# A hybrid decoder step on one core: the opening (norm, adaLN, first projections, gates) in another sequence

## The chip, the cores and the metric

The kernel runs on one core of one Trainium2 chip. The metric is device time in microseconds of one execution. The core has five engines that each work through their own queue of instructions in order: PE (matrix products), DVE and ACT (elementwise work, PSUM reads), POOL (elementwise work in SBUF) and SP (here it only issues DMAs). They wait for each other through semaphores.

## What is computed

One decoder layer over 576 tokens: a prompt of 512 and 8 samples of 8 tokens. Cut to what matters here:

```
mod = silu(c) @ ada_w + ada_b                  # 6 x 1024 per sequence
sh1, sc1, g1, sh2, sc2, g2 = split(mod, 6)
hn = rmsnorm(x, norm1_w) * (1 + sc1) + sh1
u = hn @ w_in       # z, xbc, dt, q, k, v, o, ig, fg, xr, gr
xbc = silu(causal_conv(xbc))                   # width 4
y_ssd = SSD(xbc, dt), y_ml = mLSTM(q, k, v, ig, fg), y_lru = RG-LRU(xr, gr)
x = x + g1 * (concat(y_ssd, y_ml, y_lru) @ w_out)
hn2 = rmsnorm(x, norm2_w) * (1 + sc2) + sh2
x = x + g2 * (square(relu(hn2 @ mlp_up)) @ mlp_down)
y = rmsnorm(x, final_norm_w)
```

## The kernel before

All activations lie with features on the 128 partitions: `x` is 8 tiles of 128 x 576 (k = 0..7). A float32 product is made of three fast ones: each operand is split into a high part (rounded on ACT) and a low part (the rest, on DVE or POOL), and PE adds hi·hi, lo·hi and hi·lo. With two halves of 288 columns this is 6 matmuls per weight block of 128 columns and per k; below, **product (i, k)** means these six, for the i-th of the first three weight blocks (i = 0, 1, 2 are convolution channels 8, 10 and 0) and tile k. Weight blocks are numbered in their order of use: 0 is the gates' `wg`, 1 to 3 are those three, and from 4 on each block is one *unit* of 8 products.

`start` (the opening) is recorded inside `in_order`, so on each engine its instructions stand in the order of the program text; what comes after is placed by the scheduler. The opening does this:

- Loads on SP's queue: x, the first part of `vec` (small constants), then for each q the adaLN weights `ada[q]` (four DMAs of 256 KB), with the weight blocks between them.
- Sums of squares: ACT and DVE square the x tiles, DVE adds two squares, PE sums them over the partitions (`sum_tokens`, into `ms`); warm-up matmuls (`warm`) stand between. `rstd_cols` makes the norm's factor on DVE and POOL, `rstd_bcast` (tiles `ba`, `bb`, then `rb`) spreads it.
- For each q: `ada_mm(q)` on PE (tile `adap`), a copy on ACT (`adarow`), `ada_sel(q)` on PE (tile `adas`), an add on DVE (`modt`). Then `modulate(q)` on DVE, ACT and POOL (`amp`, `x`, `hnh`, `hnl`) gives the normed tile `hn[q]` as high and low part.
- The products (i, k) in the order of the table `TODO`, with `ada_sel` and `ada_mm` of later tiles between them.
- The gates (`gates_mm`): 32 matmuls of 32 columns over the x tiles (line 429), copies `gs` on DVE and ACT, two products with a selector (line 435), then `ev_gates` (`gv` on DVE, `ic` on ACT). The convolution channels follow: `ev_conv` copies PSUM to SBUF on ACT (lines 611 to 614), ACT takes the first tap (line 620), DVE the other three (line 626), ACT and DVE the SiLU (lines 649, 651, 653; tile `xbc`).

`w_prep(b)` splits weight block b: high part `wh` on ACT, low part `wl` on DVE (on POOL for blocks 7 to 32); block 3 is split in two halves (`wt`). A unit needs a pair of PSUM banks out of two (`PG`), so unit b waits for the copies of unit b - 2. `PREP_AT` says at which k blocks 2, 3 and 4 are split.

## Time and profile before

| | |
|---|---|
| three runs | 995.92, 998.04, 1000.73 us; median 998.04 us |
| the profiled execution | 995.4 us, of which the span of the trace is 993.6 us |
| PE: span 0 to 62 us | 56.14 us busy, mean granted clock 0.92 |
| PE: 62 to 100 us | 37.08 of 38 us busy, clock 1.00 |
| DVE: 62 to 100 us | 35.95 of 38 us busy |
| PE: 100 to 150, 150 to 200, 200 to 250 us | 41.92, 46.55, 45.37 of 50 us busy |
| PE: 500 to 900 us | 400 of 400 us busy |
| DMA: 0 to 40 us | busy share 0.63 in the first 5 us, then about 1 |

The span is what the profiler recorded from the first to the last instruction; 1.8 us of the execution lie around it. The table is read by stage: the opening has PE idle time and a clock below 1, the stretch to some 300 us has waits on PE, and from 500 us on PE is busy all the time, so that what comes later shifts with the moment at which it begins.

### The profile page before, as it was taken

What the parts mean: (1) busy time and instruction counts of PE and PEld (TensorE: products, weight loads), DVE (VectorE), ACT (ScalarE), POOL (GpSimd) and SP (SyncE); (2) the same over time, 40 slices, a digit from 0 to 9 for tenths busy, and PEclk for the clock granted to TensorE, in tenths of its full rate; (3) what the DMA queues carried; (4) which work ended last, traced back from release to release, by engine and by line L of the source; (5) the groups of instructions that cost most, each with busy time, mean ns of one, the idle gap of its engine ahead of it and who ended that gap; (6) DMA issues with size and microseconds to landing.
All of it is one profiled execution on the core that took longest, in us unless ns stands there. A gap on an engine that the chain in (4) does not pass through costs nothing.

```text
span 993.6 us, 18146 instructions
## 1 busy us (share of the span) xinstructions
PE 959.5 (97%) x7369; PEld 904.1 (91%) x7370; DVE 590.2 (59%) x1180; ACT 399.8 (40%) x741; POOL 203.8 (21%) x220
## 2 busy tenths in 40 slices
PE   8999789889999999999999999999999999999996
PEld 5889778777788899999999999999999999999996
DVE  4669897887788377468444455533553355335544
ACT  3454744453646674345222234312441144114320
POOL 2836454532355532020000000000000000000032
PEclk8999999998999999999999999999999999999998
DMA  9721254654464333444222322222222222222202
GB/s 343 294 86 64 81 186 133 246 173 137 131 223 153 105 137 129 140 131 162 91 98 105 110 86 84 74 79 84 85 86 85 86 85 76 76 83 85 85 23 96
DMA packets 51220, 119.62 MB, mean 120 GB/s; under 512 B 6956, under 2 KB 17468, under 8 KB 51136
## 3 DMA queue, kind: packets, MB, share of 16 engines
q1 hardware_dynamic: 47024, 111.06, 32.7%
q10 hardware_dynamic: 3744, 6.85, 1.8%
q8 instruction: 58, 0.95, 0.4%
q0 software_dynamic: 368, 0.55, 0.2%
q14 instruction: 26, 0.21, 0.1%
HBM read 108.68 MB, written 9.76 MB: 119 GB/s over the span
## 4 chain that ended last, share of the span: by engine, by line
PE 76%; DVE 10%; ACT 4%; issue 3%; DMA 1%; POOL 0%; POOLq 0%; DVEq 0%; ACTq 0%
PE g L164 66%; DVE r L626 3%; PE adap L218 1%; PE g L1363 1%; DMA nmb<-scr_nm 1%; PE py L729 1%; PE lg L1129 1%; DVE att L707 1%; PE ps L734 1%; PE py L732 1%; DVE nmb L924 1%; DVE xbc L651 0%; DVE sp_e L494 0%; PE adas L228 0%; ACT r L620 0%
## 5 line engine op out<-in xcount | busy, mean ns | idle before, releaser
L150 ACT ACTIVATE wh<-raw 128x1024 fp32r<-128x1024 f32 x123 | 130.1, 1058 | 333.9 <-PE g L164 309.4
L164 PE MATMUL g<-hnh,wh 128*128 128x288 f32 x688 | 153.1, 302 | 10.1 <-ACT r L614 8.0
L164 PE MATMUL g<-hnh,wl 128*128 128x288 f32 x688 | 152.1, 299 | 0.6 <-DVE wl L152 0.6
L164 PE MATMUL g<-hnl,wh 128*128 128x288 f32 x688 | 151.8, 299 | 0.0
L152 DVE TENSOR_TENSOR wl<-raw,wh 128x1024 fp32r<-128x1024 f32 x97 | 118.7, 1225 | 29.5 <-ACT wh L150 29.4
L164 PEld LDWEIGHTS g<-hnh,wh 128*128 128x128 f32 x688 | 110.4, 189 | 19.3 <-ACT r L614 9.2
L164 PEld LDWEIGHTS g<-hnh,wl 128*128 128x128 f32 x688 | 111.6, 189 | 2.7 <-issue 1.2
L164 PEld LDWEIGHTS g<-hnl,wh 128*128 128x128 f32 x688 | 111.7, 189 | 0.8 <-issue 0.4
L164 PE MATMUL g<-h2h,wh 128*128 128x288 f32 (+1 forms) x512 | 110.9, 297 | 0.0
L164 PE MATMUL g<-h2l,wh 128*128 128x288 f32 (+1 forms) x512 | 110.9, 298 | 0.0
L164 PE MATMUL g<-h2h,wl 128*128 128x288 f32 (+1 forms) x512 | 110.0, 296 | 0.0
L307 DVE SCALAR_TENSOR_TENSOR xr<-g,modt,xr 128x288 f32<-128x288 f32 x38 | 19.7, 518 | 141.2 <-PE g L164 141.2
L164 PE MATMUL g<-hh,wl 128*128 128x288 f32 x480 | 102.9, 295 | 0.0
L164 PE MATMUL g<-hh,wh 128*128 128x288 f32 x480 | 102.5, 295 | 0.0
L164 PE MATMUL g<-hl,wh 128*128 128x288 f32 x480 | 102.4, 295 | 0.0
L1405 POOL TENSOR_SCALAR xr<-xr,vec 128x576 f32<-128x576 f32 (+2 forms) x8 | 15.2, 1900 | 383.8 <-ACT sqa L1237 363.4
L152 POOL TENSOR_TENSOR wl<-raw,wh 128x1024 fp32r<-128x1024 f32 x26 | 69.0, 2653 | 80.3 <-ACT wh L150 61.4
L164 PEld LDWEIGHTS g<-h2h,wl 128*128 128x128 f32 x512 | 83.4, 188 | 0.0
L164 PEld LDWEIGHTS g<-h2h,wh 128*128 128x128 f32 x512 | 83.1, 189 | 0.1
L164 PEld LDWEIGHTS g<-h2l,wh 128*128 128x128 f32 x512 | 83.0, 188 | 0.0
L164 PEld LDWEIGHTS g<-hh,wh 128*128 128x128 f32 x480 | 77.0, 188 | 0.0
L164 PEld LDWEIGHTS g<-hh,wl 128*128 128x128 f32 x480 | 77.0, 188 | 0.0
(399 smaller groups left out, 1652.7 us busy)
## 6 DMA issues: line engine op xcount, KB each, us to landing
raw<-w SPq DMA_DIRECT2D x124, 512.0 KB, 3.5
ada<-ada SPq DMA_DIRECT2D x32, 512.0 KB, 5.6
ada<-ada SPq DMA_DIRECT2D x32, 256.0 KB, 5.9
cumb<-scr_cum SPq DMA_DIRECT2D x16, 256.0 KB, 5.6
s<-s SPq DMA_DIRECT2D x16, 256.0 KB, 4.7
ssm_s<-s ACTq DMA_DIRECT2D x16, 256.0 KB, 2.9
x<-x SPq DMA_DIRECT2D x8, 288.0 KB, 4.7
xr<-x SPq DMA_DIRECT2D x8, 288.0 KB, 3.9
```

The source lines that it names most:

```text
L150: nc.scalar.activation(hi, raw, AF.Copy)
L152: eng.tensor_tensor(lo, raw, hi.bitcast(FT), op=OP.subtract)
L164: self.nc.tensor.matmul(pg.h[h][:m, :e], w(k), xx[:, h * HALF:h * HALF + e], start=start and n == 0, stop=stop and n == 2)
L218: nc.tensor.matmul(ps[32 * j:32 * j + 32, :256], self.cs[:, k, :], ks(k), start=k < 4, stop=k >= 4)
L307: self.nc.vector.scalar_tensor_tensor(dst[:, :HALF], pg.h[0][:, :HALF], gate[:, 0:1], x[:, :HALF], op0=OP.mult, op1=OP.add)
L626: nc.vector.scalar_tensor_tensor(a[:, :n], r[:, j:j + n], wcols[:, j:j + 1], a[:, :n], op0=OP.mult, op1=OP.add)
L707: self.eng("att").tensor_scalar(E[:, h * 128:(h + 1) * 128], cums[h2][:, h * 128:(h + 1) * 128], self.col1[:, c, hd:hd + 1], 0.0, op0=OP.a ...
L729: nc.tensor.matmul(o, xdt[:, h * 64:(h + 1) * 64], att[h // 4][:, hs], start=True, stop=not c)
L732: nc.tensor.matmul(o, S[:, h * 64:(h + 1) * 64], ce[h // 4][:, hs], start=False, stop=True)
L734: nc.tensor.matmul(pst, cb[:, 128:256], xend[:, :512], start=True, stop=True)
L924: self.eng("nmb").tensor_scalar(E[:, tk(c)], nmb[:, tk(c)], ecol(c), 0.0, op0=OP.add, op1=OP.min)
L1405: self.eng("fin").tensor_scalar(x, x, self.v("fnw")[:, o:o + 1], None, op0=OP.mult)
```

## The change

`start` is written in another order; no operation on the data is new except how the last pair of squares is summed.

- The last two squares (k = 6 and 7) are not added on DVE: both go to PE as sums of their own. Of 36 warm-up matmuls 24 are left: 14, 4, 4 and 2, where before there were 14, 4, 4, 4, 4 and 6.
- `rstd_cols` stands ahead of the tanh of the adaLN input; the `cs` operand is made after it.
- The split of block 1 stands ahead of `rstd_bcast`, on ACT's and on DVE's queue.
- `ada_mm` runs one q further than the product at hand instead of two, and `ada_sel(k + 1)` with `modulate(k + 1)` now stand in iteration k, behind its first product.
- Loads: `wg` and the second part of `vec` move behind all adaLN weights; blocks 1, 2 and 3 move ahead.
- `TODO` takes the channel-0 products in other portions; block 2, 3 and 4 are split one k earlier each.
- `ev_conv` of channel 8 stands behind product (0, 7), ahead of the gates; on PE the gates' second step stands further back, inside unit 5.

```diff
-            for q in range(PAIR_AT):
+            self.hn, rows = [None] * KT, {}
+            w0 = self.w_raw_gates()
+            for q in range(KT):
                 load(q)
-                self.w_load(W_AT.get(q, 0))
+                self.w_load(W_AT.get(q, -1))
+                if q == VEC_AT:
+                    nc.sync.dma_start(self.vec[:, NV1:], io["vec"][:, NV1:])
+                    w0()
...
-                nc.vector.tensor_tensor(sb, sa, sb, op=OP.add)
+                if k == KT - 2:
+                    self.sum_tokens(sa, ms, False, False)
+                else:
+                    nc.vector.tensor_tensor(sb, sa, sb, op=OP.add)
                 self.sum_tokens(sb, ms, k == 0, k == KT - 2)
-                if k < KT - 2:
+                if k < KT - 4:
                     self.warm(WARM[1])
+            r = self.rstd_cols(ms, 1.0 / D, EPS)
             th = self.rpool.tile([128, 8, 32], FT, name="cth", tag="r")
...
-            r = self.rstd_cols(ms, 1.0 / D, EPS)
...
+            self.warm(WARM[2])
             ada_mm(0)
-            self.w_prep(0)
...
+            self.w_prep(1)
             rb = self.rstd_bcast(r)
-            self.warm(WARM[2])
-            self.ada_sel(0, rows[0])
-            self.hn = [None] * KT
-            self.hn[0] = self.modulate(x[0], rb, 0)
-            self.w_prep(1)
-            self.warm(WARM[3])
+            modulation(0)
             ada_mm(1)
-            self.ada_sel(1, rows[1])
-            ada_mm(2)
             pgs = [self.PG(), self.PG(), PairTile(banks=[self.P("g"), self.P("g")])]
             for k in range(KT):
-                if k + 1 < KT:
-                    self.hn[k + 1] = self.modulate(x[k + 1], rb, k + 1)
-                if k in PREP_AT:
-                    self.w_prep(2 + PREP_AT.index(k))
...
                     if n == 0:
+                        if k + 1 < KT:
+                            modulation(k + 1)
                         if k + 2 < KT:
-                            self.ada_sel(k + 2, rows[k + 2])
-                        if k + 3 < KT:
-                            ada_mm(k + 3)
-            if not GATES_FIRST:
-                ps = self.gates_mm(x)
+                            ada_mm(k + 2)
+                        if k in PREP_AT:
+                            self.w_prep(2 + PREP_AT.index(k))
+                        if k == KT - 1:
+                            self.ev_conv(pgs[0], 8)
+            ps = self.gates_mm(x)
             self.ev_gates(ps)
-            self.ev_conv(pgs[0], 8)
...
+    def w_raw_gates(self):
+
+        t = self.T("wg")[:, :256]
+        self.w_split[0] = t.rearrange("p (k m) -> p k m", k=8)
+        self.w_next_dma = self.w_next_split = 1
+        return lambda: self.nc.sync.dma_start(t, self.io["wg"])
...
-WARM = 14, 4, 4, 6
-PAIR_AT = 3
-W_AT = {0: 1, 2: 2, 4: 3}
+WARM = 14, 4, 2
+W_AT = {0: 1, 1: 2, 3: 3}
 VEC_AT = 7
-PREP_AT = 1, 3, 6
...
+PREP_AT = 0, 2, 5
```

`modulation(q)` is `ada_sel(q)` followed by `modulate(q)`. In `TODO` the products of channel 0 (i = 2) stood two at each of k = 4 to 7; now they stand at k = 3 to 7 as one, two, two, two and one.

**PE at the first products.** This is PE's queue of before, up to the first product (0, 0) (tile `g_341`, high part `hnh_297`): `adap` is one adaLN step's product (four rows), `adas` its selection.

```order
L218 MATMUL adap_315<-ada_118,cs 32x256 x2
L218 MATMUL adap_315<-ada_119,cs 32x256 x2
L218 MATMUL adap_315<-ada_120,cs 32x256 x2
L218 MATMUL adap_315<-ada_121,cs 32x256 x2
L228 MATMUL adas_326<-vec,adarow_324 128x9 x2
L218 MATMUL adap_330<-ada_126,cs 32x256 x2
L218 MATMUL adap_330<-ada_127,cs 32x256 x2
L218 MATMUL adap_330<-ada_128,cs 32x256 x2
L218 MATMUL adap_330<-ada_129,cs 32x256 x2
L164 MATMUL g_341<-hnh_297,wh_304 128x288 x2
L164 MATMUL g_341<-hnl_298,wh_304 128x288 x2
L164 MATMUL g_341<-hnh_297,wl_305 128x288 x2
```

And this is the same place of the change, where the first product is `g_316` with `hnh_298`, and the rows behind it are iteration 0's.

```order
L216 MATMUL adap_305<-ada_117,cs 32x256 x2
L216 MATMUL adap_305<-ada_118,cs 32x256 x2
L216 MATMUL adap_305<-ada_119,cs 32x256 x2
L216 MATMUL adap_305<-ada_120,cs 32x256 x2
L162 MATMUL g_316<-hnh_298,wh_274 128x288 x2
L162 MATMUL g_316<-hnl_299,wh_274 128x288 x2
L162 MATMUL g_316<-hnh_298,wl_275 128x288 x2
L226 MATMUL adas_326<-vec,adarow_314 128x9 x2
L216 MATMUL adap_343<-ada_127,cs 32x256 x2
L216 MATMUL adap_343<-ada_128,cs 32x256 x2
L216 MATMUL adap_343<-ada_129,cs 32x256 x2
L216 MATMUL adap_343<-ada_130,cs 32x256 x2
```

The selection of tile 1 and the product of adaLN step 2 moved from ahead of product (0, 0) to behind it; the next product, (0, 1), needs that selection.

**ACT at the end of the opening.** ACT's queue of before from the split of blocks 5 and 6 (`wh_764`, `wh_768`) over the gates to the copies and the first tap of channel 8 (`g_341` is its PSUM).

```order
L150 ACTIVATE wh_764<-raw_756 128x1024
L150 ACTIVATE wh_768<-raw_758 128x1024
L433 ACTIVATE gs_693<-gp_676 128x288
L477 ACTIVATE ic_699<-gp_675,vec 4x288
L477 ACTIVATE ic_699<-gp_676,vec 4x288
L611 ACTIVATE r_707<-g_341 128x288
L613 ACTIVATE r_707<-g_341 128x224
L614 ACTIVATE r_707<-g_341 128x8x8
L620 ACTIVATE r_713<-r_707,cwh 128x600
```

The same place of the change: blocks 5 and 6 are `wh_754` and `wh_758`, channel 8 is `g_316`, channel 10 `g_317`.

```order
L148 ACTIVATE wh_754<-raw_746 128x1024
L611 ACTIVATE r_656<-g_316 128x288
L613 ACTIVATE r_656<-g_316 128x224
L614 ACTIVATE r_656<-g_316 128x8x8
L148 ACTIVATE wh_758<-raw_748 128x1024
L620 ACTIVATE r_662<-r_656,cwh 128x600
L611 ACTIVATE r_713<-g_317 128x288
```

The copies of channel 8 stand ahead of the gates, between two weight splits.

**DVE at the same place.** DVE's queue of before from the low parts of blocks 5 and 6 to the taps of channels 8 (`r_713`) and 10 (`r_729`).

```order
L152 TENSOR_TENSOR wl_765<-raw_756,wh_764 128x1024
L152 TENSOR_TENSOR wl_769<-raw_758,wh_768 128x1024
L432 COPY gs_693<-gp_675 128x288
L475 TENSOR_SCALAR gv_698<-gp_675,vec 64x288
L475 TENSOR_SCALAR gv_698<-gp_676,vec 64x288
L645 TENSOR_SCALAR cwh<-vec 128x60
L626 SCALAR_TENSOR_TENSOR r_713<-r_707,cwh,r_713 128x600 x2
L626 SCALAR_TENSOR_TENSOR r_729<-r_723,cwh,r_729 128x600
```

And of the change, with channel 8 as `r_662`, channel 10 as `r_719` and channel 0 as `r_735`.

```order
L150 TENSOR_TENSOR wl_759<-raw_748,wh_758 128x1024
L626 SCALAR_TENSOR_TENSOR r_662<-r_656,cwh,r_662 128x600 x2
L626 SCALAR_TENSOR_TENSOR r_719<-r_713,cwh,r_719 128x600
L626 SCALAR_TENSOR_TENSOR r_662<-r_656,cwh,r_662 128x600
L626 SCALAR_TENSOR_TENSOR r_719<-r_713,cwh,r_719 128x600 x2
L651 SCALAR_TENSOR_TENSOR xbc_669<-r_656,r_662 128x512
L653 SCALAR_TENSOR_TENSOR xbc_669<-r_656,r_662 128x64
L432 COPY gs_702<-gp_684 128x288
L626 SCALAR_TENSOR_TENSOR r_735<-r_729,cwh,r_735 128x600
L475 TENSOR_SCALAR gv_707<-gp_684,vec 64x288
L626 SCALAR_TENSOR_TENSOR r_735<-r_729,cwh,r_735 128x600
L475 TENSOR_SCALAR gv_707<-gp_685,vec 64x288
```

The gate copies `gs` and `gv` moved behind the six taps of channels 8 and 10, in among those of channel 0. On PE the two selector products of the gates (line 435), which stood ahead of unit 4, now stand inside unit 5, behind ten of its 24 pairs of matmuls.

More of the change, by code (lines that the diff above doesn't have):

```diff
@@ L124, in w_load @@
             b = self.w_next_dma
-            t = self.T("wg") if b == 0 else self.wpool.tile([128, 1024], FT, name=self.name("raw"), tag="raw", bufs=RAW_BUFS)
-            src = self.io["wg"] if b == 0 else self.io["w"][b - 1]
+            t = self.wpool.tile([128, 1024], FT, name=self.name("raw"), tag="raw", bufs=RAW_BUFS)
+            src = self.io["w"][b - 1]
             n = src.shape[1]
@@ L138, in w_prep @@
             m = raw.shape[2]
-            if b == 0:
-                self.w_split[b] = raw
-            elif b == 3:
+            if b == 3:
                 hl = [[self.T("wt", FR)[:, :512].rearrange("p (k m) -> p k m", k=4) for _ in range(2)] for _ in range(2)]
@@ L353, in load, with ada_mm, modulation @@
                     nc.sync.dma_start(ada[q][i][:, :512], io["ada"][q, :, i * 512:(i + 1) * 512])
-            for q in range(PAIR_AT):
-                load(q)
-                self.w_load(W_AT.get(q, 0))
+            def ada_mm(q):
+                t = ada.pop(q)
+                rows[q] = self.ada_mm(lambda k: t[k // 2][:, (k % 2) * 256:(k % 2 + 1) * 256])
+            def modulation(q):
+                self.ada_sel(q, rows.pop(q))
+                self.hn[q] = self.modulate(x[q], rb, q)
+            self.hn, rows = [None] * KT, {}
+            w0 = self.w_raw_gates()
+            for q in range(KT):
+                load(q)
+                self.w_load(W_AT.get(q, -1))
+                if q == VEC_AT:
+                    nc.sync.dma_start(self.vec[:, NV1:], io["vec"][:, NV1:])
+                    w0()
+            self.w_load(4)
+            self.start_dma = self.last()
             ms = self.P("ms")
@@ L373, in start @@
             nc.vector.scalar_tensor_tensor(self.cs, th, 1.0, ct, op0=OP.add, op1=OP.mult)
-            r = self.rstd_cols(ms, 1.0 / D, EPS)
-            rows = {}
-            def ada_mm(q):
-                t = ada.pop(q)
-                rows[q] = self.ada_mm(lambda k: t[k // 2][:, (k % 2) * 256:(k % 2 + 1) * 256])
-            ada_mm(0)
-            self.w_prep(0)
-            for q in range(PAIR_AT, KT):
-                if q == VEC_AT:
-                    nc.sync.dma_start(self.vec[:, NV1:], io["vec"][:, NV1:])
-                load(q)
-                self.w_load(W_AT.get(q, 0))
-            self.w_load(4)
-            self.start_dma = self.last()
-            rb = self.rstd_bcast(r)
-            self.warm(WARM[2])
-            self.ada_sel(0, rows[0])
-            self.hn = [None] * KT
-            self.hn[0] = self.modulate(x[0], rb, 0)
-            self.w_prep(1)
-            self.warm(WARM[3])
+            self.warm(WARM[2])
+            ada_mm(0)
+            self.w_prep(1)
+            rb = self.rstd_bcast(r)
+            modulation(0)
             ada_mm(1)
-            self.ada_sel(1, rows[1])
-            ada_mm(2)
             pgs = [self.PG(), self.PG(), PairTile(banks=[self.P("g"), self.P("g")])]
             for k in range(KT):
-                if k + 1 < KT:
-                    self.hn[k + 1] = self.modulate(x[k + 1], rb, k + 1)
-                if k in PREP_AT:
-                    self.w_prep(2 + PREP_AT.index(k))
-                if k == KT - 1 and GATES_FIRST:
-                    ps = self.gates_mm(x)
                 for n, (i, kk) in enumerate(TODO.get(k, [(0, k), (1, k), (2, k)])):
@@ L1467 @@
 ADA_WAIT, ADA_REST = 3, 1
[L1468 to L1470 removed]
+WARM = 14, 4, 2
+W_AT = {0: 1, 1: 2, 3: 3}
 VEC_AT = 7
[L1472 to L1474 removed]
+PREP_AT = 0, 2, 5
+TODO = {0: [(0, 0)], 1: [(0, 1), (1, 0), (1, 1)], 2: [(0, 2), (1, 2)], 3: [(0, 3), (1, 3), (2, 0)], 4: [(0, 4), (1, 4), (2, 1), (2, 2)], 5: [(0, 5), (1, 5), (2, 3), (2, 4)]}
+TODO[6] = [(0, 6), (1, 6), (2, 5), (2, 6)]
+TODO[7] = [(0, 7), (1, 7), (2, 7)]
 LOOKAHEAD = 4
```

3 lines of the change are left out of this document (removed).

## The prediction

> **What bounds the kernel now.** I read the page first, then the chain of waits, then PE's timeline. The page's span, its busy times and the engines' shares of the chain that ended last:
>
> ```profile
> span 993.6 us, 18146 instructions
> ...
> PE 959.5 (97%) x7369; PEld 904.1 (91%) x7370; DVE 590.2 (59%) x1180; ACT 399.8 (40%) x741; POOL 203.8 (21%) x220
> ...
> PE 76%; DVE 10%; ACT 4%; issue 3%; DMA 1%; POOL 0%; POOLq 0%; DVEq 0%; ACTq 0%
> ```
>
> PE bounds the kernel as a whole, yet the chain is not PE's everywhere. In order of time (start, us, what) it runs behind the opening through the convolution's taps and the gates on DVE, and joins PE again at 142.91 us. The windows row gives PE's and DVE's busy time in the first part of that stretch, and the two timeline rows PE's waits at its head and at its worst:
>
> ```profile
> 61.46 0.85 DVE r L626
> ...
> 142.91 1.05 PE ps L734 x2
> 62.00:103.00 41.00, 37.08 (x279) 36.62 (x277) 38.95 (x50) 21.31 (x41) 21.53 (x27) 1.00 0.18 65
> 60.51 0.54 PE L164 MATMUL g<-hnh,wh 128*128 128x288 f32 x2 [2.10 <-ACT r L614]
> 103.65 0.70 PE L164 MATMUL g<-hnh,wh 128*128 128x288 f32 x2 [4.28 <-ACT r L614]
> ```
>
> DVE works 38.95 of those 41.00 us, while PE waits 4.28 us at 103.65 for copies that stand behind it. So two moments set the end: when unit 4 begins on PE (60.51), and, ahead of it, when DVE's taps begin (**61.46**). PE's later begin alone costs nothing until 4.28 us are used up. Behind 142.91 the order of work is nearly unchanged and PE is busy, so what the opening gains there arrives at the end one to one.
>
> **Up to the first product.** PE's timeline of before:
>
> ```profile
> 11.48 0.44 PE L442 MATMUL warm<-wz 128*128 128x512 bf16 x1
> 12.13 1.06 PE L442 MATMUL warm<-wz 128*128 128x512 bf16 x2 [0.22 <-issue]
> 12.99 2.00 PE L270 MATMUL ms<-ones,r 128*128 128x1 f32 x10
> 14.92 1.93 PE L218 MATMUL adap<-ada,cs 128*32 128x256 f32 x16
> 16.78 1.12 PE L278 MATMUL ba<-vec,col 128*128 128x128 f32 x4
> 24.86 0.54 PE L164 MATMUL g<-hnh,wh 128*128 128x288 f32 x2
> 17.00:18.00 1.00, 1.00 (x5) 0.67 (x4) 0.00 (x0) 0.37 (x2) 0.00 (x0) 0.50 1.05 404
> ```
>
> The last warm-up group begins at 11.48 and with the last sum ends at 14.99. In its place stand two sums; most of both falls under the half clock that the last row shows (0.50). 2 x 2.00 less what the first instructions gain gives 15.3: DVE's saved addition lay beside PE's warm-up and buys nothing. Two warm-ups (1.06) bring adaLN step 0 to 16.2 (before 14.92), its end to 18.1, and ba, bb and the selection to 19.4, adaLN step 1 to 20.4. ACT and DVE now split block 1 first. Their rows, and those of the rest of a tile's chain:
>
> ```profile
> 16.92 0.38 ACT L220 ACTIVATE adarow<-adap 128x256 f32<-128x256 f32 x1 [4.96 <-PE adap L218]
> 17.93 0.60 ACT L282 ACTIVATE rb<-ba 128x512 f32<-128x512 f32 x1 [0.63 <-PE ba L278]
> 21.96 1.04 ACT L150 ACTIVATE wh<-raw 128x1024 fp32r<-128x1024 f32 x1
> 37.10 0.72 ACT L298 ACTIVATE hnh<-x,modt 128x512 fp32r<-128x512 f32 x1 [0.41 <-DVE x L293]
> 50.84 1.23 DVE L152 TENSOR_TENSOR wl<-raw,wh 128x1024 fp32r<-128x1024 f32 x1 [0.72 <-ACT wh L150]
> 24.54 0.16 DVE L229 TENSOR_TENSOR modt<-adas,vec 128x18 f32<-128x18 f32 x1
> 25.00 0.75 DVE L293 SCALAR_TENSOR_TENSOR x<-x,amp,rb 128x512 f32<-128x512 f32 x1
> 26.54 0.75 DVE L300 SCALAR_TENSOR_TENSOR hnl<-x,modt,hnh 128x512 fp32r<-128x512 f32 x1 [0.79 <-ACT hnh L298]
> ```
>
> adarow to 18.5, wh to 19.5, rb to 20.2; wl 19.5 to 20.7; from modt's begin to x's end it took 1.21 (24.54 to 25.75), here 1.4 with the gaps between engines, to 22.1; hnh to 22.9. Product (0, 0) begins at **22.9**, 1.96 us earlier.
>
> **The loop.** One selection, one adaLN product and one product's six matmuls (44.87 to 45.66, 0.79 us), by start to start:
>
> ```profile
> 34.67 0.51 PE L228 MATMUL adas<-vec,adarow 128*128 128x9 f32 x4
> 35.11 1.07 PE L218 MATMUL adap<-ada,cs 128*32 128x256 f32 x16
> 36.11 0.53 PE L164 MATMUL g<-hnh,wh 128*128 128x288 f32 x2
> ...
> 44.87 0.42 PE L164 MATMUL g<-hnh,wh 128*128 128x288 f32 x2
> ...
> 45.66 0.51 PE L228 MATMUL adas<-vec,adarow 128*128 128x9 f32 x4
> 51.67 0.42 PE L164 MATMUL g<-hnh,wh 128*128 128x288 f32 x2
> 54.93 2.15 PE L429 MATMUL gp<-x,wg 128*32 128x288 f32 x32
> 57.19 1.21 PE L435 MATMUL gp<-gs,vec 128*96 128x288 f32 x4
> ```
>
> So 0.44, 1.00, 0.79. From a selection's end to the next tile's hnh it takes 1.21 + 0.72 with gaps, 2.1 us, and to hnl 0.8 more, of which the first two matmuls cover 0.27. Before, this lay behind a whole iteration; now PE has only the adaLN product and the iteration's other products (none, two, one, two at k = 0 to 3) to fill it. Step by step: (0, 0) waits for its hnl and ends 24.25; selection and adaLN product to 25.7; hnh of tile 1 at 26.8, PE idle 1.1. (0, 1) to 28.15; tile 2's modt stands behind block 2's wl until 29.45, hnh 31.5, idle 0.3. (0, 2) to 32.85; hnh of tile 3 at 35.45, idle 0.35. (0, 3) to 36.8; tile 4's modt behind the two lows of block 3 until 38.2, hnh 40.3, idle 0.45. (0, 4) to 41.6. From there three products cover the chain and PE is full: (0, 5) at 45.45, (0, 6) at 50.1, (0, 7) at 53.75 to 54.55, the loop's end 56.15. Before these were 52.46 (51.67 + 0.79) and 54.93. The five waits for hnl (0.55 each) and the idle make 4.95 us, more than the earlier begin.
>
> The clock adds to it. Before, it was at 0.50 in two stretches, the second as the second of these rows shows:
>
> ```profile
> 23.32 0.61 PE L228 MATMUL adas<-vec,adarow 128*128 128x9 f32 x4 [1.33 <-ACT adarow L220]
> 26.00:28.00 2.00, 2.00 (x18) 1.46 (x20) 1.39 (x4) 0.66 (x2) 1.55 (x3) 0.50 1.05 381
> ```
>
> It followed a stretch whose longest PE gap was the 1.33 us of the first row; the change has one of 2.5 us (20.4 to 22.9). If 22 to 25.5 us falls to half, selection 1 and its neighbours cost 0.6 us more in the chain, and (0, 7) ends at 55.15. The Trainium skill, TensorE: Matmul & The Clock Gate, section Why this matters for your kernels, asks only for no PE-idle gaps over some 3 us between bursts; by that the clock stays full, and (0, 7) ends at 54.55. The half clock of 17 to 18 us, with PE busy 1.00 of 1.00 us, goes against taking idle gaps as all that counts. I take the middle of the two ends, **54.85**.
>
> **Loads.** Of every adaLN group the last issue moves to the same place in SP's queue or earlier, since wg is out of the way; the second part of vec and wg go late, just ahead of block 4. SP's issue of block 4, and wg's size and time to landing:
>
> ```profile
> 33.64 0.33 SPq L128 DMA_DIRECT2D raw<-w  x1
> wg<-wg SPq DMA_DIRECT2D x1, 128.0 KB, 6.0
> ```
>
> So wg lands by 40 us and is first read after the loop: it costs nothing; without the loop over it a late wg would hold the gates.
>
> **The end of the opening.** ACT's and DVE's rows of before:
>
> ```profile
> 59.67 0.41 ACT L611 ACTIVATE r<-g 128x288 f32<-128x288 f32 x1
> 60.53 0.89 ACT L620 ACTIVATE r<-r,cwh 128x600 f32<-128x600 f32 x1
> 56.68 0.46 DVE L432 COPY gs<-gp 128x288 f32<-128x288 f32 x1 [0.83 <-PE gp L429]
> 57.96 1.17 DVE L475 TENSOR_SCALAR gv<-gp,vec 64x288 f32<-64x288 f32 x2 [0.82 <-PE gp L435]
> 68.58 2.42 DVE L651 SCALAR_TENSOR_TENSOR xbc<-r,r 128x512 f32<-128x512 f32 x1 [1.50 <-ACT r L649]
> ```
>
> Channel 8's taps now need, from the end of (0, 7): block 5's wh (1.04), the copies (59.67 to 60.53, 0.85), block 6's wh (1.04), ACT's tap (0.89) beside block 6's wl (1.23): 4.1 us with gaps, where it was 61.46 - 52.46 = 9.0. Taps begin at 54.85 + 4.1 = **58.95, 2.5 us earlier**. Against that, gs and gv (0.46 + 1.17 = 1.63), which lay before the taps beside PE's gates, now stand among them in DVE's full stretch: -1.63. And channel 0's first tap comes late: six taps and channel 8's xbc took 61.46 to 67.08 (68.58 less its 1.50), so they end at 64.6, and gs at 65.0; from 64.6 on, when their buffer is free, channel 0's copies run on ACT (0.85), then block 7's wh (1.04), which now stands between the copies and the tap, then the tap (0.89): 67.4. DVE waits 2.4 us, where before it waited 1.50 at the same place: -0.9. Behind that tap DVE's first gv waits for the gates' product inside unit 5: unit 4 begins at 56.15 + 2.15 = 58.3 and takes 24 x 0.265 = 6.4, ten pairs of unit 5 take 2.65, half of the product's 1.21 leads to 68.0, when the tap is still running. Bounds for DVE's wait here, which the trace does not show: none (the queues drift so that it is hidden) and 3.0 (68.0 - 65.0), if the tap comes early and only the product holds it; I take 2.4, since ACT's rows give it.
>
> Sum: 2.5 - 1.63 - 0.9 = **0.0 us**. PE's own path gains 2.2 at unit 4 (58.3 against 60.51) less the 1.2 us of the gates' second product that it runs later, but waits at 103.65 for DVE all the same. The profiled execution (993.6 of span, 1.8 around it) stays at 995.4; it lies 2.64 below the median of the three runs, so against these I say **998 us**.
>
> **Rivals.** *The chain is hidden* (faster): if the loop's 4.95 us of waits fall away but for 1 us, taps begin at 55.0, 6.4 earlier, and the sum is 6.4 - 1.63 - 0.9 = 3.9: 994.1. For it: the rows of DVE and ACT are short, and PE's order could absorb 0.55 per wait. Against: before, no product came sooner than these rows allow. All 4.95 and no wait of DVE gives 2.5 + 4.95 - 1.63 + 1.5 = 7.3, 990.7. *The clock stays at half* (slower): the sums and (0, 0) to (0, 2) come with gaps in every stretch; if 22 to 36 us all run at half, six products, four selections and three adaLN products (9.5 us) take some 8 more (1.93 against 1.07 for the adaLN product), of which the 3.9 us of waiting there hide half: (0, 7) is 4.1 later, 1002.1; it decides for the worse once it holds past 26 us, and two more such stretches at the same rate bring 1004. For it: the 0.50 at 26 to 28 followed smaller gaps. Against: the idle is spread over the stretch in pieces of half a microsecond, and from k = 4 PE is full. *The tail gives nothing* (no change, the change not doing what it says): the gates' product on PE waits in its turn for gs, which stands behind DVE's six taps, and DVE's gv behind it loses another 2 us: 1000. For it: PE cannot pass the product. Against: gs is done at 65.0, and PE comes there at 67.4.
>
> **How the numbers follow.** Forecast 998 with 0.63; hidden chain 0.20; half clock 0.10; empty tail 0.07. Half of the hidden chain passes 0.5% (5 us, about what a measurement of this kernel can tell from no change), and some of the forecast's cases do by luck of the order behind the opening, where single waits of PE are worth up to 4.28: faster 0.15. Of the half clock most of its upper end and as much from that order: slower 0.09. Same 0.76. The range takes in the bounds of DVE's wait (2.4 better, 0.6 worse), most of the hidden chain and of the half clock: 991.5 to 1003.
>
> **What would show it.** Product (0, 0) near 22.9; PE idle ahead of (0, 1) to (0, 4), released by ACT's hnh and DVE's hnl; (0, 7) done at 54.5 to 55.2; the first tap near 59; DVE waiting at gv or at channel 0's tap; PE's wait at 103.65 still some 4 us. A first tap at 56 or before, or one after 61.5, would make the prediction wrong, as would a changed sum of PE's waits from 62 to 250 us.

## The result and the profile after

The change is slower: 1003.39 us (median of 20 runs, 999.85 to 1005.09) against 995.76 us (20 runs, 992.72 to 1000.87) of the kernel before on the same chip, a ratio of 1.0062 with a 95% interval of 1.0047 to 1.0077. (The ratio, like those below, weighs the runs in its own way and is not the plain quotient of the two medians, which is 1.0077.) The medians lie 7.6 us apart where the forecast's sum had 0.0, and 1003.39 us is 0.4 us above the range forecast. The profiled execution took 1004.41 us against 995.4. Its page has the same shape as before, PE 97% busy and the chain of waits divided in the same way, only longer:

```profile
span 1002.6 us, 18150 instructions
...
PE 968.8 (97%) x7368; PEld 913.2 (91%) x7368; DVE 591.3 (59%) x1179; ACT 398.5 (40%) x741; POOL 203.1 (20%) x220
...
PE 77%; DVE 10%; issue 3%; ACT 3%; POOL 1%; DMA 1%; POOLq 0%; DVEq 0%; SPq 0%; ACTq 0%
```

The places that the prediction named stand in PE's timeline of the change (start, us, what, and in brackets the idle time ahead of it with what ended it): the sums, adaLN step 0, product (0, 0), the product behind (0, 7), and the first products of units 10 and 11 (two consecutive units of the convolution stretch, each waiting for the copies of the unit that held its PSUM pair).

```profile
11.58 6.19 PE L268 MATMUL ms<-ones,r 128*128 128x1 f32 x30
18.67 1.94 PE L216 MATMUL adap<-ada,cs 128*32 128x256 f32 x16
25.41 0.85 PE L162 MATMUL g<-hnh,wh 128*128 128x288 f32 x2 [0.65 <-ACT hnh L296]
...
60.81 0.42 PE L162 MATMUL g<-hnh,wh 128*128 128x288 f32 x2
109.58 0.85 PE L162 MATMUL g<-hnh,wh 128*128 128x288 f32 x2 [5.10 <-ACT r L614]
122.21 0.53 PE L162 MATMUL g<-hnh,wh 128*128 128x288 f32 x2 [4.16 <-ACT r L614]
```

Product (0, 7) is done at 60.81, 6 us later than forecast. The windows rows say why: the second number is PE's busy time in the stretch, the granted clock is the third number from the right.

```profile
11.00:25.00 14.00, 13.77 (x75) 9.51 (x73) 3.00 (x9) 2.29 (x5) 2.90 (x4) 0.50 1.03 396
25.00:37.00 12.00, 11.38 (x61) 8.14 (x62) 5.89 (x10) 4.00 (x10) 9.17 (x12) 0.50 1.05 399
37.00:38.00 1.00, 1.00 (x8) 1.00 (x8) 0.00 (x0) 0.00 (x0) 0.85 (x2) 0.80 1.01 413
38.00:60.00 22.00, 21.30 (x187) 17.87 (x185) 12.37 (x24) 7.41 (x17) 16.59 (x23) 1.00 0.30 116
```

From 11 to 37 us PE has work for 25.15 of 26 us and runs all of it at 0.50. Before, the rows at 0.50 lay at 12 to 18 and 26 to 28 us. On DVE the first tap comes 3.8 us behind (0, 7), as forecast, and the copies of the gates and channel 0's late tap stand where the prediction put them:

```profile
64.59 4.86 DVE L626 SCALAR_TENSOR_TENSOR r<-r,cwh,r 128x600 f32<-128x600 f32 x6
70.11 0.45 DVE L432 COPY gs<-gp 128x288 f32<-128x288 f32 x1
72.84 2.31 DVE L626 SCALAR_TENSOR_TENSOR r<-r,cwh,r 128x600 f32<-128x600 f32 x1 [2.28 <-ACT r L620]
75.07 0.56 DVE L475 TENSOR_SCALAR gv<-gp,vec 64x288 f32<-64x288 f32 x1
```

So at the first tap the change is 3.1 us behind (64.59 against 61.46), at unit 10 it is 5.9 behind (109.58 against 103.65), and at unit 11 it is 8.5 behind (122.21 against 113.74). At the end it is 9.0 behind. In between the lag is not steady: at the `ps` matmuls where the prediction let the chain join PE (142.84 us in before's timeline) it is down to 6.8 us. Three questions followed: why the clock was low, what makes the lag grow behind the first tap, and how much each is worth.

### The profile page after: what moved, and what is told of

It is laid out like the page before. It is cut to its first block, busy times and chain, and to the rows that moved or that the text cites. A ratio compares the mean times of both kernels' runs of the same rounds, so it can differ in the third digit from the quotient of the medians.

```text
span 1002.6 us, 18150 instructions
## 1 busy us (share of the span) xinstructions
PE 968.8 (97%) x7368; PEld 913.2 (91%) x7368; DVE 591.3 (59%) x1179; ACT 398.5 (40%) x741; POOL 203.1 (20%) x220
## 3 DMA queue, kind: packets, MB, share of 16 engines
q1 hardware_dynamic: 47024, 111.06, 32.5%
## 4 chain that ended last, share of the span: by engine, by line
PE 77%; DVE 10%; issue 3%; ACT 3%; POOL 1%; DMA 1%; POOLq 0%; DVEq 0%; SPq 0%; ACTq 0%
PE g L162 67%; DVE r L626 3%; PE adap L216 1%; PE g L1363 1%; PE py L729 1%; PE lg L1129 1%; PE ps L734 1%; DMA nmb<-scr_nm 1%; DVE att L707 1%; PE py L732 1%; PE pn L971 0%; DVE nmb L924 0%; DVE nmb L929 0%; PE adas L226 0%; PE pu L829 0%
## 5 line engine op out<-in xcount | busy, mean ns | idle before, releaser
L162 PE MATMUL g<-hnh,wh 128*128 128x288 f32 x688 | 156.3, 306 | 12.3 <-ACT r L614 9.4
L162 PE MATMUL g<-hnl,wh 128*128 128x288 f32 x688 | 154.6, 304 | 0.7 <-DVE hnl L298 0.7
L162 PEld LDWEIGHTS g<-hnh,wh 128*128 128x128 f32 x688 | 112.7, 192 | 23.9 <-ACT r L614 10.1
L162 PEld LDWEIGHTS g<-hnh,wl 128*128 128x128 f32 x688 | 113.8, 193 | 1.1 <-issue 0.4
L150 POOL TENSOR_TENSOR wl<-raw,wh 128x1024 fp32r<-128x1024 f32 x26 | 64.7, 2489 | 77.0 <-ACT wh L148 51.0
```

The lines of the kernel that those rows point to most:

```text
L150: eng.tensor_tensor(lo, raw, hi.bitcast(FT), op=OP.subtract)
L162: self.nc.tensor.matmul(pg.h[h][:m, :e], w(k), xx[:, h * HALF:h * HALF + e], start=start and n == 0, stop=stop and n == 2)
```

## The experiments

Sixteen kernels ran, each timed in five rounds against before. The table holds them all. The half clock is worked out from windows rows of 1 us between 9 and 42 us, as 2 x (1 - granted clock), summed; the mean clock is the mean, over a kernel's executions, of the clock over the whole span. Times of the profiled execution are starts in its trace; "(0, 7) done" is the start of the next product. One profile is one execution, so its columns go together, and the ratio speaks for all executions.

| kernel | ratio to before (95%) | mean clock | half clock, us | (0, 0) | (0, 7) done | first tap |
|---|---|---|---|---|---|---|
| before | 1 | 0.986 | 10.3 | 24.86 | 52.45 | 61.46 |
| the change | 1.0062 (1.0047 to 1.0077) | 0.978 | 27.3 | 25.41 | 60.81 | 64.59 |
| e8: the change again | 1.0063 (1.0040 to 1.0087) | 0.977 | 13.7 | 22.92 | 56.44 | 60.21 |
| e1: change, 36 warm-ups | 1.0055 (1.0032 to 1.0078) | 0.981 | 10.2 | 24.83 | 57.35 | 61.12 |
| e2: before, 24 warm-ups | 1.0022 (1.0000 to 1.0044) | 0.980 | 17.1 | 25.13 | 52.88 | 61.89 |
| e3: change, gates first | 1.0065 (1.0037 to 1.0093) | 0.980 | 20.5 | 22.60 | 58.71 | 66.90 |
| e4: before, early copies and taps | 1.0021 (0.9997 to 1.0044) | 0.984 | 10.3 | 24.43 | 51.98 | 55.77 |
| e5: change, two-ahead pairing | 1.0071 (1.0045 to 1.0097) | 0.977 | 13.7 | 27.37 | 56.63 | 60.40 |
| e6: before, early copies only | 1.0049 (1.0023 to 1.0074) | 0.982 | 0.0 | 22.53 | 50.34 | 55.41 |
| e7: change, early copies only | 1.0116 (1.0084 to 1.0148) | 0.978 | 27.3 | 25.42 | 60.78 | 65.93 |
| e9: change, order pinned | 1.0038 (1.0017 to 1.0058) | 0.979 | 20.5 | 22.60 | 57.58 | 61.33 |
| e10: before, the change's order | 1.0044 (1.0020 to 1.0068) | 0.982 | 10.2 | 24.90 | 52.49 | 61.49 |
| e11: e4, order pinned | 1.0009 (0.9987 to 1.0030) | 0.984 | 13.7 | 27.02 | 54.63 | 58.41 |
| e12: e6, order pinned | 0.9970 (0.9950 to 0.9990) | 0.987 | 17.1 | 28.12 | 56.99 | 62.06 |
| e13: e9 with 36 warm-ups | 0.9998 (0.9979 to 1.0016) | 0.988 | 13.6 | 27.03 | 59.58 | 63.35 |
| e14: before, one-ahead pairing | 1.0048 (1.0026 to 1.0070) | 0.983 | 13.6 | 23.82 | 57.79 | 66.78 |
| e15: before, new front part | 1.0020 (0.9998 to 1.0042) | 0.984 | 13.7 | 27.45 | 56.36 | 65.36 |
| e16: e12 with 52 warm-ups | 0.9981 (0.9959 to 1.0004) | 0.991 | 0.0 | 25.02 | 52.82 | 57.88 |

**The warm-ups (e1, e2).** Each kernel got the other's warm-up matmuls; DVE's, ACT's and POOL's rows keep their order.

```diff
-                if k < KT - 4:
+                if k < KT - 2:
                     self.warm(WARM[1])
...
-            self.warm(WARM[2])
             ada_mm(0)
             self.w_prep(1)
             rb = self.rstd_bcast(r)
+            self.warm(WARM[2])
             modulation(0)
+            self.warm(WARM[3])
...
-WARM = 14, 4, 2
+WARM = 14, 4, 4, 6
```

> The change with before's 36 warm-up matmuls in before's places (14, 4, 4, 4 between the sums, 4 behind ba and bb, 6 behind the selection of tile 0), the two ahead of adaLN step 0 gone; DVE's, ACT's and POOL's order is that of the change throughout. Theory A (the removed warm-ups are what keeps PE at 0.50 from 10.5 to 37 us): half clock ends by 22 us, but may fall back for some us near 26; product (0,0) near 24.7, the loop then takes the 31.7 us that the prediction worked out for full clock, (0,7) done near 56.4 instead of 60.8, first tap near 60.3 (after 64.59), time about 999 us (4 us below the change). Rival B (the one-ahead adaLN order makes the loop this long, the clock hides in its waits): full clock returns but (0,7) is done at 59 or later and the time stays within 1.5 us of the change, 1002 to 1004.

> Before with the change's 24 warm-up matmuls (14, 4, 4, and 2 ahead of adaLN step 0), nothing else; DVE's, ACT's and POOL's order is that of before throughout. Theory A: clock at 0.50 from about 11 us to 30 us or beyond, (0,7) done 3 to 5 us later than 52.46, first tap 3 to 5 us later than 61.46, time 998.5 to 1001 us. Rival B (the two-ahead order needs no warm-ups, its loop is fed densely enough): half clock ends before 26 us as in before, (0,7) within 1.5 us of 52.46, time 995 to 997 us.

In e1 the clock is full from 22 us on, and (0, 0) to (0, 7) takes 32.5 us (24.83 to 57.35; the change 35.4). That is the loop at full clock, 0.9 us above the 31.65 of the prediction. Theory A was right about the clock, yet the time hardly moved (1.0055): the first tap came even before that of before, and behind it, up to 280 us, 6.9 us were lost. In e2 the half clock grew to 17.1 us, as theory A said, but moved (0, 7) by 0.4 us only, as rival B said; before's pairing hides it. The ratio still rose by 0.22%. So the clock alone was not the answer, and what is lost behind the first tap was larger than I had put it.

**The tail (e3, e4).** The copies and taps of channel 8 were moved alone, out of the change (e3) and into before (e4).

```diff
-                        if k == KT - 1:
-                            self.ev_conv(pgs[0], 8)
             ps = self.gates_mm(x)
             self.ev_gates(ps)
+            self.ev_conv(pgs[0], 8)
```

> The change, but with the copies and taps of channel 8 behind the gates as in before: behind the opening DVE, ACT and PE stand again in before's order. Theory A (early copies bring the first tap 5 us forward, and cost 1.63 for gs and gv, 0.9 for channel 0's tap and, by the other order that the scheduler makes behind them, another 2.6 at units 10 and 11): the first tap comes 9.0 us behind the end of (0,7), at 69.5, 8 us later than before's 61.46, and PE's waits near 115 us shrink to before's size; time 1003 to 1004.5 us, as the change. Rival C (the tail is what costs, and the opening's loss is hidden by the wait at 103.65): first tap near 69.5 too, but the time falls to 997 to 999 us.

> Before, with the copies and taps of channel 8 ahead of the gates as in the change, nothing else in the opening. Theory A: first tap 3.8 to 4.1 us behind (0,7), at 56.4 instead of 61.46; -5.1, +1.63 for gs and gv, +0.9 for channel 0's tap, so 2.6 faster where the scheduler's order behind it stays as in before (993.2 us), and nothing (995.8 us) if it makes the waits of units 10 and 11 that the change shows. Rival D (the tail's edit loses by itself): 998 us or more.

In e4 the first tap came 3.8 us behind (0, 7), 5.7 us earlier than before, and nothing of it was left: 1.0021 (median 999.43 us), as rival D had it. In e3 the first tap came 8.2 us behind (0, 7), and the time stayed that of the change. What early copies gain at the first tap they lose behind it (in e4 6.1 us up to 280 us); that is more than the 2.5 us which gs, gv and channel 0 account for.

**The pairing, a lighter tail, and the change again (e5 to e8).** e5 gives the change before's two-ahead pairing; e6 and e7 move only ACT's part of channel 8 ahead of the gates; e8 is the change once more.

```diff
+            self.ada_sel(1, rows[1])
+            ada_mm(2)
...
+                if k + 1 < KT:
+                    self.hn[k + 1] = self.modulate(x[k + 1], rb, k + 1)
...
-                        if k + 1 < KT:
-                            modulation(k + 1)
                         if k + 2 < KT:
-                            ada_mm(k + 2)
+                            self.ada_sel(k + 2, rows[k + 2])
+                        if k + 3 < KT:
+                            ada_mm(k + 3)
```

> The change with before's pairing of adaLN and products (adaLN two steps further than the product at hand, the selection an iteration ahead of its product); its 24 warm-ups, its sums, loads and tail stay, and DVE's order behind the opening is that of the change. Theory A (the one-ahead pairing costs 4.9 us of the loop at full clock, and through it the half clock costs 3 more): half clock lasts to 28 us or beyond as in the run of before with 24 warm-ups, yet (0,7) is done 27.6 us (full clock) to 28.5 behind the first product, at 52 to 53.7; first tap 3.8 us later, 56 to 57.5; with the 5.6 to 6.9 us that the early copies' order lost behind the first tap so far, 994.5 to 998 us by before's profiled 995.4, 996 to 999.5 by its median. Rival B (the half clock alone makes the loop long): (0,7) done at 57 or later, 1000 us or more.

```diff
+                        if k == KT - 1:
+                            head = self.ev_conv_head(pgs[0], 8)
...
             self.ev_gates(ps)
-            self.ev_conv(pgs[0], 8)
+            self.ev_conv_tail(8, *head)
```

> Before, with only ACT's part of channel 8 (three copies and the first tap) ahead of the gates; DVE's three taps stay behind the gates' first copy gs in the program text, and gv follows them by the scheduler. Theory A (the loss of the early copies is that gs, gv and the gates' chain stand behind two channels' taps on DVE): channel 8's taps run in DVE's gaps around gs and gv, DVE is 2.4 us further at 61.5 than before, PE's wait at 103.65 shrinks to 1.9 us or moves up by as much: 993 to 994.5 us. Rival E (any other order that the scheduler makes behind the opening loses about as much as the early copies gain): 996 us or more, with waits of 3 us and more at units 10 and 11.

> The change, with DVE's taps of channel 8 behind the gates' copy gs and only ACT's part ahead of the gates. Theory A: the opening's loss stays ((0,7) done 58.5 to 61), the first tap comes about 5 us behind that, but behind it nothing is lost against before but 1 us: 998.5 to 1001 us, 3 us below the change. Rival E: 1002 us or more.

> The change itself once more, for a second profile of its clock and for a time on the same chip as the three runs beside it. Theory A: half clock of 14 us or more in all between 10 and 38 us, in one stretch or in two, (0,7) done at 58.5 to 61, first tap 3.8 us behind; 1002 to 1004 us. Rival F (the half clock of 26.8 us was an accident of one profiled execution): half clock of 10 us or less, (0,7) done at 57.5 or before.

None of the three edits was faster, and e7 was worst (1.0116). e5 shortened the loop to 29.3 us (27.37 to 56.63), but began it late and lost 10.2 us from the first tap to 280 us. e6 had no half clock in the opening at all and its first tap at 55.41, and was still slower than before, as rival E had it for the time; PE's longest wait there stands at 143.99 us, 5.43 us for DVE's `att`, where before waits 1.27. e8 showed two things. The same program had 13.7 us of half clock this time, in two stretches, a little less than theory A's 14 and more than rival F's 10. (0, 7) was done at 56.44, as rival F had it, and the first steps fell where the prediction put them: adaLN step 0 at 16.18, (0, 0) at 22.92. But its time did not follow its profile (999.27 us was the lowest of its 12 runs; median 1004.18). And between the first tap and unit 11 it lost what the first profile lost: 117.82 - 60.21 = 57.6 us, and 122.21 - 64.59 = 57.6, where before took 52.3. A loss that comes back to 0.1 us in two executions with different clocks points to the order of the work, and the next runs put that to the test.

**The order behind the opening, pinned (e9 to e12).** What is recorded behind the opening is the same list of instructions in both kernels; only the scheduler's order on each engine differs. So I chained these instructions, engine by engine and as far as the two orders differ, in the order that they have in one kernel, and let the other kernel's opening stand ahead of them. `PINNED` holds for each engine the instructions' numbers in the wanted order.

```diff
+def pin(tc, insts):
+    for runs in PINNED.values():
+        row = []
...
+        for p, i in zip(row, row[1:]):
+            tc.add_manual_dep(i, p.name, mybir.DependencyInfo(mybir.DependencyClass.NoSync,
+                                                              mybir.DependencyReason.DATA), reason="pin")
...
+        pin(tc, list(tc.nc.cur_bb.bb.instructions)[k.n_start:])
```

> The change, with every instruction that is recorded behind the opening pinned, engine by engine, to the order in which it stands in before; the opening (its gates and channel 8 too) stays the change's. Theory G (the scheduler's new order behind the opening costs 2 to 3 us, above all at units 10 and 11): from the first tap to 280 us the kernel loses 2.5 to 3 us against before, where the two profiles of the change lose 4.8 and 5.6; PE's wait at unit 11 is 1.5 us instead of 3.2 to 4.2; 1000.5 to 1002 us. Rival H (that order costs nothing; clock and opening are all): the loss behind the first tap stays at 4.8 or more, 1003 to 1005 us.

> Before, opening untouched, with every instruction recorded behind the opening pinned to the order in which it stands in the change. Theory G: the first tap stays at 61.5 (by the clock's luck 1 us more or less), PE's wait at unit 11 grows from 1.36 to 3.5 us or more and 2 to 3 us are lost by 280 us: 998.5 to 1000 us. Rival H: 995.5 to 997.5 us, as before.

> Before with channel 8's copies and taps ahead of the gates (as in the run with early copies), and all that is recorded behind the opening pinned to before's order. Theory G: first tap near 55.8, of which 2.5 to 3 us are lost to gs, gv and channel 0's first tap, nothing more: 2.6 to 3.2 us below before, 993 to 994.5 us. Rival H: as the run with early copies, 998 us or more.

> Before with only ACT's part of channel 8 ahead of the gates, and all that is recorded behind the opening pinned to before's order. Theory G: DVE is 2.4 us further than before once channel 8's and 10's taps are done, and keeps that: 993 to 995 us. Rival H: as the same edit without the pinned order, 1000 us or more.

e10 is the cleanest: before's opening, with its first tap at 61.49, and only the change's order behind it. Unit 10 begins at 103.69, as before (103.65); unit 11 at 116.31, 2.6 us later; and the kernel is 0.44% slower (0.20 to 0.68). Its timeline shows why unit 11 comes late, on ACT:

```profile
105.92 0.68 ACT L553 ACTIVATE d<-cs 4x576 f32<-4x576 f32 x1
...
113.64 0.67 ACT L568 ACTIVATE em<-mt 4x576 f32<-4x576 f32 x1
114.22 0.29 ACT L569 ACTIVATE it<-mx 4x128 f32<-4x128 f32 x1
114.53 1.06 ACT L150 ACTIVATE wh<-raw 128x1024 fp32r<-128x1024 f32 x1
115.50 0.39 ACT L611 ACTIVATE r<-g 128x288 f32<-128x288 f32 x1
```

and on DVE:

```profile
107.10 0.75 DVE L541 TENSOR_TENSOR cs<-de,sp 16x576 f32<-16x576 f32 x1
107.88 0.84 DVE L626 SCALAR_TENSOR_TENSOR r<-r,cwh,r 128x600 f32<-128x600 f32 x1
108.76 0.17 DVE L554 TENSOR_TENSOR d<-cs,vec 4x8 f32<-4x8 f32 x1
108.96 0.84 DVE L626 SCALAR_TENSOR_TENSOR r<-r,cwh,r 128x600 f32<-128x600 f32 x1
109.83 1.35 DVE L555 TENSOR_TENSOR_SCAN mx<-d,d 4x576 f32<-4x576 f32 x1
111.21 0.84 DVE L626 SCALAR_TENSOR_TENSOR r<-r,cwh,r 128x600 f32<-128x600 f32 x1
```

The scan `mx` opens the mLSTM gate rows `nm`, `mo`, `em`, `it` on ACT, and behind these, in ACT's queue, stand the copies (L611) for which unit 11 waits. In the change's order two taps (L626) stand ahead of `mx` on DVE and a third behind it, and on ACT a weight split (`wh`, 1.06 us) stands ahead of the copies. Ahead of these taps, at 105.08, the copy `d` (L551) takes 1.97 us in e10 where before takes 0.16; the last section comes back to it. In before the same places read, on DVE and ACT:

```profile
106.17 1.35 DVE L555 TENSOR_TENSOR_SCAN mx<-d,d 4x576 f32<-4x576 f32 x1
107.55 2.81 DVE L626 SCALAR_TENSOR_TENSOR r<-r,cwh,r 128x600 f32<-128x600 f32 x1
...
112.77 0.26 ACT L599 ACTIVATE col<-cb 64x128 f32<-64x128 f32 x1
112.93 0.40 ACT L611 ACTIVATE r<-g 128x288 f32<-128x288 f32 x1
```

There `mx` comes first, with one tap behind it, and no weight split stands directly ahead of the copies at 112.93; in e10 they run at 115.50, 2.6 us later.

Most of these 2.6 us are paid back, though. Before waits at 132.82 (1.53 us) and at 142.47 (1.27 us) for DVE's `att`; e10 has only 0.38 us of this, at 143.33, and is 0.86 us behind at `ps`. What lasts is lost at 200 us. These are `ps`, the products `pi` and an adaLN product on PE, the additions `y` on DVE and a weight's low part on POOL, in before:

```profile
142.84 1.13 PE L734 MATMUL ps<-xend,cbm 128*128 128x512 f32 x2
195.63 2.35 POOL L152 TENSOR_TENSOR wl<-raw,wh 128x1024 fp32r<-128x1024 f32 x1
196.41 2.94 DVE L848 TENSOR_TENSOR y<-y,cump 128x64 f32<-128x64 f32 x4
199.67 0.71 PE L1003 MATMUL pi<-C,q 128*128 128x130 f32 x4 [0.85 <-DVE C L985]
207.22 1.07 PE L218 MATMUL adap<-ada,cs 128*32 128x256 f32 x16
```

and in e10:

```profile
143.70 1.12 PE L734 MATMUL ps<-xend,cbm 128*128 128x512 f32 x2
196.40 4.52 DVE L848 TENSOR_TENSOR y<-y,cump 128x64 f32<-128x64 f32 x4
197.50 2.35 POOL L152 TENSOR_TENSOR wl<-raw,wh 128x1024 fp32r<-128x1024 f32 x1
201.24 0.71 PE L1003 MATMUL pi<-C,q 128*128 128x130 f32 x4 [2.91 <-DVE C L985]
210.30 1.07 PE L218 MATMUL adap<-ada,cs 128*32 128x256 f32 x16
```

In the change's order POOL's weight split runs later, beside more of `y`, which takes 4.52 us instead of 2.94. `C` stands behind `y` on DVE, so PE waits 2.91 us for it, and then the granted clock is 0.51 from 202.5 to 206 us, where before has no half clock. From there e10 stays 3.1 us behind up to some 500 us. The change and its second profile have the same wait (2.92 and 2.93 us). Their lag on before, in us, by the places in before:

| | first tap | unit 11 | `ps`, 142.84 | `adap`, 207.22 | end of the span |
|---|---|---|---|---|---|
| the change | 3.1 | 8.5 | 6.8 | 9.1 | 9.0 |
| e8: the change again | -1.3 | 4.1 | 3.4 | 4.2 | 3.9 |
| e10: before, the change's order | 0.0 | 2.6 | 0.9 | 3.1 | 4.0 |
| e9: change, order pinned | -0.1 | 3.1 | 3.1 | 4.6 | 5.1 |

From `ps` to `adap` e8 loses 0.8 us where the change loses 2.3: its clock stays at 1.00 behind that wait (203 to 210 us).

In e9 the change with before's order takes 55.5 us from the first tap to unit 11 (61.33 to 116.84) instead of 57.6, and 1.0038. Theory G held for e10, and in part for e9, whose intervals with the change overlap and which lost 4.8 us to 280 us instead of 3; some 1.5 us of that, between `ps` and `adap`, are not explained. e11 fell short of its 993 to 994.5 us: its first tap came 3 us earlier than before's, which was used up at unit 11 (113.64), and 1.4 us more were lost between 142 and 280 us. e12 turned 1.0049 into 0.9970, with the same opening: **faster than before**, by 0.3% (0.1 to 0.5), and at 996.19 us (before on its chip: 998.29) still short of theory G's 993 to 995.

**What the opening costs (e13 to e16).** With before's order pinned everywhere, e13 restores the warm-ups in the change (the diff of e1), e14 puts the one-ahead pairing alone into before (the diff of e5 backwards), e15 the front part alone:

```diff
-                nc.vector.tensor_tensor(sb, sa, sb, op=OP.add)
+                if k == KT - 2:
+                    self.sum_tokens(sa, ms, False, False)
+                else:
+                    nc.vector.tensor_tensor(sb, sa, sb, op=OP.add)
...
+            r = self.rstd_cols(ms, 1.0 / D, EPS)
             th = self.rpool.tile([128, 8, 32], FT, name="cth", tag="r")
...
+            self.w_prep(1)
             rb = self.rstd_bcast(r)
```

and e16 is e12 with `WARM = 14, 6, 4, 6, 4`, the second number behind all four sums and the last behind adaLN step 1.

> The change with before's 36 warm-ups in before's places and all behind the opening pinned to before's order. Theory A+G (missing warm-ups and the scheduler's order are two losses that add): first product near 24.8, (0,7) near 57.3, first tap near 61.1, 3 us lost behind it; mean clock 0.983; 998 to 1000.5 us, within 0.3% of before. Rival J (the two are one loss: each alone gives what both give): as the pinned change, 1001.5 us or more, 0.35% above before or more.

> Before with the change's one-ahead pairing of adaLN and products, warm-ups, sums, loads and tail as before, and all behind the opening pinned to before's order. Theory A (the pairing lengthens the loop by 4.9 us and begins it up to 2 us earlier): first product 22.5 to 24, (0,7) done 55 to 56.5, first tap 64 to 65.5, 2.5 to 4 us slower than before: 0.25 to 0.4%. Rival K (what the two-ahead order saves in the loop it pays ahead of it): (0,7) within 1 us of 52.5, time within 0.1% of before.

> Before with the change's front part alone: the last two squares go to PE as sums of their own, the norm's factor stands ahead of the tanh, block 1 is split ahead of the factor's spreading; 36 warm-ups, pairing and tail as before, order behind the opening pinned to before's. Theory A (ten more small sums on PE cost 1.2 to 2 us there and DVE's saved addition buys nothing; PE, not ACT, holds the first product): first product 1 to 2 us later than 24.9, 0.1 to 0.2% slower. Rival L (the front part is what the change gains): first product at 24 or before, 0.1% faster or more.

> The run that was faster than before (ACT's part of channel 8 ahead of the gates, order pinned) with more warm-ups: 14, then 6 behind each of the four sums, 4, 6 and 4 (48 in all). Theory A (dense warm-ups hold the clock): half clock of 6 us or less between 10 and 38 us, mean clock 0.990, 0.3 to 0.6% below before. Rival M (the half clock comes whatever PE does there, or the extra matmuls cost what it gives): mean clock 0.987 as without them, 0.3% below before or less.

e13 is level with before (0.9998; medians 998.89 and 997.42 us), though the warm-ups alone left 1.0055 and the order alone 1.0038. The two together are the change's loss, as far as a kernel without both shows it. e14: the pairing moves (0, 7) by 5.3 us and costs 0.48%, more than theory A's 0.25 to 0.4. e15: the front part costs 0.2%, at the edge of what the runs can tell. e16 has 52 warm-ups (14, four times 6, 4, 6 and 4), not the 48 of its expectation. It held the clock at 1.00 up to 42 us in its profile and has the highest mean clock, but is not faster than e12; whether the extra matmuls cost what the clock gives, two intervals that overlap do not tell. In each pair that differs in the warm-ups alone, the kernel with more of them has the higher mean clock: 0.981 (e1) against 0.978 and 0.977 of the change, 0.986 against 0.980 (e2), 0.988 (e13) against 0.979 (e9), 0.991 (e16) against 0.987 (e12). The parts do not add up (e14 and e15 alone would make e13 slower than before; their taps stand behind the gates, e13's don't), and how they combine stays open.

## Why the prediction was wrong, point by point

- **Up to the first product: right, where the clock allowed it.** 22.9 was forecast; 22.92 in the second profile of the change, 22.60 in e3 and e9, 25.41 in the first profile, where the sums and adaLN step 0 ran late at half clock. But the gain of 1.96 us rested on one profile of before: with its front unchanged, the same step lay at 24.86 there, and at 24.43, 22.53, 24.90, 27.02 and 28.12 us in e4, e6, e10, e11 and e12. So it moves by more than the gain with no edit ahead of it, from 22.53 with no half clock to 28.12 behind 13.7 us of it.
- **The loop: right.** 31.65 us were worked out at full clock; e1 and e13, whose half clock ends before the loop, took some 32.5 each, 4.9 us more than before's 27.6, and the waits had been put at 4.95. They were spread otherwise: in e1 PE waited at most 0.24 us for `hnl`, not 0.55.
- **The clock: the first step that failed.** The prediction took the middle of two ends, 54.55 and 55.15, and gave "the clock stays at half" a chance of 0.10 and 4.1 us at (0, 7). The first profile was that rival, to 37 us and with 6 us. Its argument against the rival, that the idle was spread in pieces of half a microsecond, does not hold: PE was 97% busy from 11 to 37 us, waited 0.65 us at most, and stayed at 0.50. Over all executions the mean clock fell from 0.986 to 0.978 (over the whole span, so with the steps behind later waits). What that is worth depends on the order behind it: with the warm-ups given back, 1.0062 became 1.0055 (e1), but with before's order pinned 1.0038 became 0.9998 (e9, e13). The Trainium skill, TensorE: Matmul & The Clock Gate, section Why this matters for your kernels, asks for no idle gaps of PE over some 3 us; taken for all that counts, this gave a full clock here. The trace does not agree.
- **Loads: right.** In the first profile the waits on PE from 18 to 62 us (engine, line, released by, us in total, times, longest) are these two, and no DMA is among them:

```profile
PE g L162 <- ACT hnh L296: 1.0, 3, 0.6
PE g L162 <- DVE hnl L298: 0.7, 3, 0.2
```

  Before's order of loads in the changed kernel was not tried by itself.
- **The end of the opening: right.** From (0, 7) to the first tap 3.8 us (4.1 forecast). For gs, gv and channel 0's tap 2.53 us were set; up to unit 10 the change loses 2.8 (5.93 - 3.13), and 2.8 in its second profile (1.55 + 1.25). DVE waited 2.28 us at channel 0's tap (2.4).
- **Behind the opening: the second step that failed.** "Behind 142.91 the order of work is nearly unchanged and PE is busy, so what the opening gains there arrives at the end one to one." The order ahead of 142.91 was compared only at the end of the opening. The scheduler changed it at 104 to 123 us as well, and there 2.5 us were lost between units 10 and 11, of which the change had 1.7 back at `ps`. Behind 142.91 the order changed too, and PE is not busy throughout (46.55 and 45.37 of 50 us from 150 to 250 us in before). From `ps` to the adaLN product at 207.22 us the change lost 2.3 us, its second profile 0.8 and e10 2.2, behind the wait for `C`. The sign that the prediction had named showed it: from 62 to 250 us PE's waits for the copies (L614) came to 9.4 us instead of 5.9. e10 shows that the new order by itself costs 0.44%, which the prediction had only as a case of luck. It was in the sum at zero.

So the terms that were worked out from rows came out within 1 us where the clock was full. The two that were not worked out are the clock of a stretch that changes its mix of matmuls and the order that a scheduler makes behind the edit; where both are put back, the loss is gone (e13). Why the pairing's later (0, 7) costs nothing there, and 0.48% in e14, stays open.

## What to carry to other kernels

Where a scheduler places the work behind an edit, compare its order on every engine as far as it differs, and not only up to the next long wait, since a lag there can be paid back and a later one stay. Pin it before judging the edit: the same edit was 0.5% slower with the order that it triggered and 0.3% faster with the old one. A matmul that computes nothing can still carry the clock for those behind it, so count it as cover until a run without it says otherwise. Profile a kernel twice before explaining half a per cent by one trace.
